# The modulated input of layer 1, made by pairs of token tiles within layer 0's output projection

## The chip, the core and the metric

The kernel runs on one core of one Trainium2 chip. The metric is the device time of one execution in microseconds, as the median of several runs. A profiled execution gives a trace in which TensorE is PE (with its weight loads as PEld), VectorE is DVE, ScalarE is ACT, GpSimd is POOL and SyncE is SP, which issues most DMAs.

## What is computed

Two layers of a hybrid diffusion backbone work on 256 context tokens and 512 latent tokens of width 1024. All is float32. Of the reference, this is what matters here:

```python
def modulate(x, shift, scale):
    return layer_norm(x) * (1.0 + scale) + shift

def hybrid_layer(x, ctx, c, c_ctx, ada_w, ada_b, in_w, ...):
    shift_l, scale_l, gate_l = jnp.split((silu(c) @ ada_w + ada_b)[:, None, :], 3, axis=-1)
    shift_c, scale_c, gate_c = jnp.split(silu(c_ctx) @ ada_w + ada_b, 3, axis=-1)
    pl = split_cols(modulate(x, shift_l, scale_l) @ in_w, IN_SPLITS)
    pc = split_cols(modulate(ctx, shift_c, scale_c) @ in_w, IN_SPLITS)
    ...                                   # four mixers, latent and context
    x_new = post_norm(ALPHA * x + gate_l * merge_branches(outs_l, ..., out_w), ln_g, ln_b)
    ...                                   # the same for the context, in layer 0
    return x_new, ctx_new
```

`merge_branches` ends with `y @ out_w`, the output projection. `post_norm` is a LayerNorm with gain and bias. So at the border of the two layers each token goes through: output projection, gate, residual, LayerNorm with gain (the new x), a plain LayerNorm, scale and shift (the modulated input), and then the first projection of layer 1.

## The kernel before

The 768 tokens are six tiles of 128 (`h[0]` to `h[5]`); tiles 0 and 1 are context (segment 0), tiles 2 to 5 latent (segment 1), and the two segments have their own scale, shift and gate. Each matmul of two float32 operands is made as three, of a high part and a low part of each (hi x hi, hi x lo, lo x hi; `mm3`, L302).

The border of the layers runs as follows.

- `out_operands` splits the merged `y` into 16 tiles `xh` of 128x768: eight high parts (ACT) and eight low parts (DVE). The first is `ys[0]`, the second `ys[1]`.
- `out_proj` goes over the six token tiles. For each it makes two halves of 512 columns, of 24 matmuls 128x512 each, in a PSUM bank of the pool `A`; DVE multiplies by the gate (L1525), adds the residual (L1526) and takes statistics (L1528).
- After a tile's two halves come `first(t)` and `second(t-1)`. `first` is the post-LayerNorm: aggregation (L309, L311), a reciprocal root by integer steps on DVE (L270 to L277), two passes of DVE over 128x1024 (L433, L434), and a store of the new x by SP (L1684). `second` is the plain LayerNorm of the tile before: statistics (L426), the same chain, `lnnb` (L430), and one in-place pass of ACT (L431).
- Then, behind the last tile, `make_xhat` runs for each of eight blocks d of 128 channels: six transposes by PE (L601) into two banks, a modulate of the context half on DVE (L462) and of the latent half on ACT (L465), and the split into high and low part (copy on DVE L479 or ACT L476, subtract on DVE L480 or POOL L477). The results are new tiles, `xh` for the 512 latent tokens and `xc` for the 256 context tokens.
- Between those, the last two of six adaLN blocks of layer 1 (numbers 4 and 5, the gate's part) are made: `ada` loads four weight tiles per block (L387), multiplies each (L392), copies the sum to SBUF (ACT, L397, tile `E`), transposes it by four small matmuls (L400) and adds the bias (DVE, L404). `ada` is a generator with five steps per block; `LEAD` says how many steps go first, and how many after each d.
- Layer 1 then begins with the projection `m_stream` (L572), whose weight tiles `wx` are split on ACT (L292) and DVE (L295).

The order of work on each engine is set by a scheduler from the program's order and its buffers; each engine then runs its own list in order. Tiles `wx` have five buffers, which adaLN loads and projection weights share.

Of the kernel before, what the change touches and what calls it, by code (L numbers as in the profile page):

```python
# [18 lines left out]
DEPTH = 2  # L19
# [15 lines left out]
LEAD = (6, 1, 6)  # L35
# [177 lines left out]
class _Kernel:  # L213
# [241 lines left out]
    def make_xhat(self, d, xn, ad, mp):  # L455
# [11 lines left out]
        out = []  # L467
        for _ in range(2):
            if self.xc is None:
                out.append(self.t(self.xp, [128, T], "xh", F32R))  # L470
            else:
                out.append((self.t(self.xc, [128, CTX], "xc", F32R), self.t(self.xp, [128, LAT], "xh", F32R)))
        for s in [slice(0, T)] if self.xc is None else [slice(0, CTX), slice(CTX, T)]:
            h, lo = (self.xtok(x, s) for x in out)
            if d % 2:
                nc.scalar.activation(out=h, in_=m[:, s], func=AF.Copy)  # L476
                nc.gpsimd.tensor_tensor(out=lo, in0=m[:, s], in1=h.bitcast(F32), op=ALU.subtract)  # L477
            else:
                nc.vector.tensor_copy(h, m[:, s])  # L479
                nc.vector.tensor_tensor(out=lo, in0=m[:, s], in1=h.bitcast(F32), op=ALU.subtract)  # L480
        self.xh.append(out[0])
        self.xl.append(out[1])

    @staticmethod
    def xtok(x, s):

        if not isinstance(x, tuple):
            return x[:, s]
        return x[0][:, s] if s.start < CTX else x[1][:, s.start - CTX:s.stop - CTX]
# [1045 lines left out]
def _run_layers(K, only=None):  # L1535
# [4 lines left out]
    xst, xct = ExitStack(), ExitStack()  # L1540
    K.xp, K.xc = xst.enter_context(mk("xh0", 16)), None
# [12 lines left out]
    for l in range(DEPTH):  # L1554
# [55 lines left out]
        xct.close()  # L1610
# [64 lines left out]
        with K.psum(A=(1, 8)):  # L1675
# [10 lines left out]

            def second(t):
                if not last:
                    K.normalise(h[t], 1e-6)
# [3 lines left out]
            if not last:  # L1693
                vec, ad = nxt["vec"], nxt["ad"]
                K.xh, K.xl = [], []
                xst.close()
                K.xp = xst.enter_context(mk(f"xh{l + 1}", 16))
                K.xc = xct.enter_context(mk(f"xc{l + 1}", 16)) if l + 1 == DEPTH - 1 else None
                with mk(f"xn{l}") as xp:
                    more = K.ada(l + 1, ad, vec, xp, range(4, 6))  # L1700
                    for _ in range(LEAD[0]):
                        next(more)
                    for d in range(8):
                        K.make_xhat(d, xn, ad, xp)
                        for _ in range(LEAD[1]):
                            next(more, None)
# [24 lines left out]
```

## Time and profile before

| | us |
|---|---|
| median of three timed runs | 2080.67 |
| lowest, highest | 2078.30, 2081.94 |
| profiled execution | 2077.99 |
| its span in the trace | 2076.2 |
| tile 3's first matmul of layer 0's output projection | at 1139.42 |
| tile 5's first matmul | at 1161.54 |
| end of tile 5's matmuls | at 1172.69 |
| first matmul of layer 1's first projection | at 1202.39 |

Times inside an execution count from the start of the span. "Busy" is time in which an engine executes; a bracket after an instruction of the trace tells how long its engine had been idle and what it had waited for. The granted clock of PE is a share of its full speed: 1.00 is 2.4 GHz, 0.50 is 1.2 GHz.

### The profile page before, as it was taken

How to read it: one execution, taken by the hardware profiler on the slowest of the kernel's cores; microseconds unless marked ns; L12 is line 12 of the kernel's file. 1: busy time of each engine (PE TensorE's matmuls, PEld its weight loads, DVE VectorE, ACT ScalarE, POOL GpSimd, SP SyncE). 2: the span in 40 equal slices, each digit the busy share in tenths (PEclk: the TensorE clock that was granted, in tenths of full speed). 3: DMA queues.
4: the chain of work that ended last, by engine and by line, in shares of the span. 5: the costliest groups of instructions: out<-in, count | busy, mean ns of one | idle time of the engine just before them, and what ended most of it. 6: DMA issues, size and time to landing. Idle time of an engine off the chain costs nothing. (4 is left out here: it accounts for less than half of the span.)

```text
span 2076.2 us, 46214 instructions
## 1 busy us (share of the span) xinstructions
PE 1900.8 (92%) x19886; PEld 1580.3 (76%) x19886; DVE 1156.2 (56%) x2471; ACT 816.1 (39%) x1649; POOL 180.3 (9%) x303
## 2 busy tenths in 40 slices
PE   6899999888899999999788879999988999999877
PEld 4778978667789998888676677878877777777556
DVE  5554453576434433443878865453686444455677
ACT  3354463565423332332122236463575333333220
POOL 1000000001200000000130010000102000000130
PEclk9899999998899999999999988999999999999999
DMA  7110123220222222223743220111102222232651
GB/s 277 43 31 29 57 87 96 78 67 22 62 79 74 81 73 73 73 73 119 252 147 115 100 66 21 43 43 31 43 21 80 78 93 79 78 91 75 217 184 41
DMA packets 62613, 176.03 MB, mean 85 GB/s; under 512 B 7448, under 2 KB 12232, under 8 KB 62408
## 3 DMA queue, kind: packets, MB, share of 16 engines
q1 hardware_dynamic: 47144, 139.93, 21.4%
q10 hardware_dynamic: 13824, 27.90, 3.9%
q0 software_dynamic: 1440, 5.24, 0.6%
q8 instruction: 156, 2.56, 0.5%
q14 instruction: 49, 0.40, 0.1%
HBM read 145.50 MB, written 27.55 MB: 83 GB/s over the span
## 5 line engine op out<-in xcount | busy, mean ns | idle before, releaser
L302 PE MATMUL ps<-xh,wx 128*128 128x384 f32 (+2 forms) x3096 | 691.7, 368 | 4.5 <-issue 1.8
L302 PEld LDWEIGHTS ps<-xh,wx 128*128 128x128 f32 x3096 | 532.1, 189 | 65.7 <-issue 8.3
L292 ACT ACTIVATE wx<-wx 128x1024 fp32r<-128x1024 f32 (+2 forms) x94 | 98.3, 1046 | 303.5 <-PE ps L302 212.3
L295 DVE TENSOR_TENSOR wx<-wx,wx 128x1024 fp32r<-128x1024 f32 (+2 forms) x94 | 113.5, 1207 | 140.9 <-ACT wx L292 138.8
L650 DVE TENSOR_REDUCE nmax<-ps 128x1 f32<-128x768 f32 (+1 forms) x160 | 134.6, 846 | 56.7 <-PE ps L647 55.7
L572 PE MATMUL ps<-wx,xh 128*128 128x256 f32 (+1 forms) x1200 | 156.4, 289 | 7.6 <-DVE mu L1001 6.7
L572 PEld LDWEIGHTS ps<-wx,xh 128*128 128x128 f32 x1200 | 151.9, 192 | 9.6 <-ACT xc L476 6.7
L302 PE MATMUL ps<-xh,wb 128*128 128x384 f32 (+1 forms) x576 | 131.5, 379 | 28.7 <-DVE th L1484 20.7
L539 PE MATMUL ps<-wx,xh 128*128 128x256 f32 x960 | 141.1, 301 | 14.6 <-DVE oth L1418 7.3
L647 PE MATMUL ps<-qk,qk 128*128 128x384 f32 (+1 forms) x504 | 134.9, 371 | 17.1 <-ACT E L653 16.9
L653 ACT ACTIVATE E<-ps,nmax 128x768 f32<-128x768 f32 (+1 forms) x160 | 130.3, 816 | 45.4 <-DVE nmax L650 41.6
L539 PEld LDWEIGHTS ps<-wx,xh 128*128 128x128 f32 x960 | 129.7, 203 | 20.2 <-DVE oth L1418 7.7
L302 PEld LDWEIGHTS ps<-xh,wb 128*128 128x128 f32 x576 | 105.6, 198 | 51.3 <-DVE th L1484 15.3
L671 ACT ACTIVATE PH<-ps 128x512 f32<-128x512 f32 x156 | 91.1, 596 | 73.4 <-PE ps L669 72.9
L647 PEld LDWEIGHTS ps<-qk,qk 128*128 128x128 f32 x504 | 83.9, 195 | 40.8 <-ACT E L653 28.4
L669 PE MATMUL ps<-cstalways,E 128*128 128x128 f32 x624 | 102.6, 287 | 2.6 <-ACT PH L671 1.4
L1444 ACT ACTIVATE mth<-ps,hmb 128x384 f32<-128x384 f32 (+1 forms) x96 | 58.5, 609 | 112.7 <-PE ps L302 111.1
L669 PEld LDWEIGHTS ps<-cstalways,E 128*128 128x128 f32 x624 | 76.5, 147 | 16.6 <-ACT PH L671 5.2
L694 PE MATMUL ps<-PH,V 128*64 128x256 f32 x624 | 84.3, 397 | 3.7 <-ACT PH L671 3.4
L629 DVE TENSOR_TENSOR qk<-ps,qk 32x256 fp32r<-32x256 f32 (+5 forms) x104 | 59.3, 575 | 43.4 <-ACT qk L628 41.7
L295 DVE TENSOR_TENSOR wx<-wf,wx 128x1024 fp32r<-128x1024 f32 (+2 forms) x34 | 40.0, 1178 | 62.4 <-PE ps L302 33.8
L694 PEld LDWEIGHTS ps<-PH,V 128*64 128x64 f32 x624 | 40.5, 139 | 34.6 <-ACT PH L671 13.4
(325 smaller groups left out, 2784.5 us busy)
## 6 DMA issues: line engine op xcount, KB each, us to landing
wx<-in_inw_dram SPq DMA_DIRECT2D x88, 512.0 KB, 3.7
wf<-in_inw_dram SPq DMA_DIRECT2D x30, 512.0 KB, 3.6
wf<-in_adaw_dram SPq DMA_DIRECT2D x24, 512.0 KB, 3.5
gd<-mth ACTq DMA_DIRECT2D x32, 384.0 KB, 2.6
th<-gd SPq DMA_DIRECT2D x32, 384.0 KB, 3.1
adaw<-in_adaw_dram SPq DMA_DIRECT2D x16, 512.0 KB, 10.2
wx<-in_outw_dram SPq DMA_DIRECT2D x16, 512.0 KB, 4.8
wb<-in_brw_dram SPq DMA_DIRECT2D x32, 256.0 KB, 3.6
```

The source lines that it names most:

```text
L292: nc.scalar.activation(out=hi[:, :n], in_=raw[:, :n], func=AF.Copy)
L295: eng.tensor_tensor(out=lo[:, :n], in0=raw[:, :n], in1=hi[:, :n].bitcast(F32), op=ALU.subtract)
L302: self.nc.tensor.matmul(o, lhsT=w, rhs=x[:, s] if s is not None else x, start=first and p == 0, stop=last and p == 2)
L539: self.nc.tensor.matmul(ps[:, j * n:j * n + n], lhsT=self.xtok(x[k], s), rhs=w, start=k == 0 and p == 0 and j == 0, stop=k == 7 and p == 2 ...
L572: self.nc.tensor.matmul(ps, lhsT=self.xtok(x[k], s), rhs=w[:, c], start=k == 0 and p == 0 and head, stop=k == 7 and p == 2 and (tail or t ...
L629: nc.vector.tensor_tensor(out=lo[r, s], in0=ps[r], in1=hi[r, s].bitcast(F32), op=ALU.subtract)
L647: nc.tensor.matmul(o, lhsT=qt[:n, q], rhs=kt[:n, s], start=i == 0, stop=i == len(passes) - 1)
L650: nc.vector.tensor_reduce(out=nm, in_=v, axis=AX.X if ctx else AX.XY, op=ALU.max, negate=True)
L653: nc.scalar.activation(out=self.halves(e[:, :n], v), in_=v, func=AF.Exp, bias=nm, accum_out=den)
L669: nc.tensor.transpose(pt[:, c:c + 128], e[:, (k0 + k) * 128:(k0 + k) * 128 + 128], self.ident)
L671: nc.scalar.activation(out=hi, in_=pt, func=AF.Copy)
L694: nc.tensor.matmul(po[64 * (kk % 2):64 * (kk % 2) + 64, :n], lhsT=v2(kk), rhs=x[:, s], start=j == 0 and k < 2, stop=j == len(groups) - 1 a ...
```

## The change

`make_xhat` no longer runs at the border. In its place `xhat_pair` makes the modulated input of two token tiles at once, and is called in `second(t)` for each odd t: for tiles 0 and 1 after tile 2's matmuls, for 2 and 3 after tile 4's, for 4 and 5 at the end. For each block d it makes two transposes (now L608), one modulate on ACT (128x256, L485) into a tile `mt` of four buffers, a copy on ACT (L489; on DVE, L487, for the last pair) and a subtract on POOL (L490; on DVE for odd d of the last pair). The results are written into the columns of `ys` that this pair's output projection has already read, so no new tiles are made, and the pools `xh1` and `xc1` are gone. The adaLN blocks 4 and 5 are stepped in `second`, three steps at a time, in a PSUM bank of their own (`D`), and the output projection of layer 0 keeps seven banks in `A`. `make_xhat` is left for layer 0's input alone, where it does what it did. Lines below L490 stand seven further down in the changed kernel (L572 is L579).

```diff
-LEAD = (6, 1, 6)
+LEAD = (0, 3, 6)
...
+    def xhat_pair(self, tt, xn, ad, mp, xh, xl, end):
+
+        nc = self.nc
+        i = 0 if tt[0] < NCT else 1
+        s = slice(tt[0] * 128, tt[-1] * 128 + 128)
+        for d in range(8):
+            ps, _ = self.tok_T(lambda t: xn[t][:, d * 128:(d + 1) * 128], 128, tt, "A")
+            m = self.t(mp, [128, 256], "mt", bufs=4)
+            nc.scalar.activation(out=m, in_=ps, func=AF.Identity, scale=ad[:, 2 * d, i:i + 1], bias=ad[:, 2 * d + 1, i:i + 1])
+            if end:
+                nc.vector.tensor_copy(xh[d][:, s], m)
             else:
...
+                nc.scalar.activation(out=xh[d][:, s], in_=m, func=AF.Copy)
+            (nc.vector if end and d % 2 else nc.gpsimd).tensor_tensor(out=xl[d][:, s], in0=m, in1=xh[d][:, s].bitcast(F32),
+                                                                      op=ALU.subtract)
...
-        with K.psum(A=(1, 8)):
+        with K.psum(**(dict(A=(1, 8)) if last else dict(A=(1, 7), D=(1, 1)))):
+            xp = None if last else mkr(f"xn{l}")
             ys = K.out_operands(y, len(qt) * 128)
...
+            if last:
+                more = None
+            else:
+                more = K.with_bank(K.ada(l + 1, nxt["ad"], nxt["vec"], xp, range(4, 6)), "D")
+
             def second(t):
-                if not last:
-                    K.normalise(h[t], 1e-6)
+                if last:
+                    return
+                K.normalise(h[t], 1e-6)
+                end = t == qt[-1]
+                for _ in range(LEAD[1] if t else 0):
+                    next(more, None)
+                if t % 2:
+
+                    K.xhat_pair((t - 1, t), xn, nxt["ad"], xp, *ys, end)
             with mk(f"ow{l}") as owp:
                 ws.append(K.out_weights(l, 1, owp))
                 K.out_proj(ys, ws, qt, gates_, h, first, second)
             if not last:
+                run(more)
                 vec, ad = nxt["vec"], nxt["ad"]
-                K.xh, K.xl = [], []
-                xst.close()
-                K.xp = xst.enter_context(mk(f"xh{l + 1}", 16))
-                K.xc = xct.enter_context(mk(f"xc{l + 1}", 16)) if l + 1 == DEPTH - 1 else None
-                with mk(f"xn{l}") as xp:
-                    more = K.ada(l + 1, ad, vec, xp, range(4, 6))
-                    for _ in range(LEAD[0]):
-                        next(more)
-                    for d in range(8):
-                        K.make_xhat(d, xn, ad, xp)
-                        for _ in range(LEAD[1]):
-                            next(more, None)
-                    run(more)
+                K.xh, K.xl = ys
```

How the instructions stand on the engines, in three places. In each row the tile written stands left of the arrow, the tiles read right of it; `ow0hi`, `ow1lo` and the like are the output projection's weights, `cstalways` holds the identity for transposes, `cs` the conditioning vectors, and the numbers behind a name tell its buffers apart.

On PE, from the end of tile 2 to the beginning of tile 3 of the output projection, the kernel before has:

```order
L302 MATMUL ps_2078_12685<-ow1hi_2049_12469,xh_2025_12415 128x512
L302 MATMUL ps_2078_12685<-ow1lo_2050_12470,xh_2025_12415 128x512
L302 MATMUL ps_2078_12685<-ow1hi_2049_12469,xh_2026_12416 128x512
L302 MATMUL ps_2091_12758<-ow0hi_2028_12423,xh_2011_12387 128x512
L302 MATMUL ps_2091_12758<-ow0lo_2029_12424,xh_2011_12387 128x512
```

The last two rows are tile 3's. The changed kernel has at the same place:

```order
L302 MATMUL ps_2078_12691<-ow1hi_2049_12475,xh_2026_12422 128x512
L392 MATMUL ps_2090_12763<-wx_2091_12764,cs_45_118 32x256 x4
L608 MATMUL ps_2092_12770<-cstalways_43_113,h0_1850_11641 128x128
...
L392 MATMUL ps_2090_12763<-wx_2140_13042,cs_45_118 32x256 x4
L400 MATMUL ps_2142_13050<-sum4_46_121,E_2141_13048 128x2 x4
L392 MATMUL ps_2174_13217<-wx_2175_13218,cs_45_118 32x256 x4
...
L400 MATMUL ps_2202_13324<-sum4_46_121,E_2201_13322 128x2 x4
...
L608 MATMUL ps_2106_12819<-cstalways_43_113,h1_1851_11643 128x128
L302 MATMUL ps_2109_12827<-ow0hi_2028_12429,xh_2011_12393 128x512
```

Both adaLN blocks and all 16 transposes of tiles 0 and 1 have moved between tile 2 and tile 3. Tile 3's first bank is one that the second L485 has read.

On ACT, from the plain LayerNorm of tile 0 on, the kernel before has:

```order
L431 ACTIVATE h0_1850_11641<-h0_1850_11641,lnnb_2074_12652,lnrs_2072_12639 128x1024
L431 ACTIVATE h1_1851_11643<-h1_1851_11643,lnnb_2089_12754,lnrs_2087_12741 128x1024
L431 ACTIVATE h2_1852_11645<-h2_1852_11645,lnnb_2104_12856,lnrs_2102_12843 128x1024
L431 ACTIVATE h3_1853_11647<-h3_1853_11647,lnnb_2119_12958,lnrs_2117_12945 128x1024
L397 ACTIVATE E_2167_13179<-ps_2141_13097 128x512
```

and the changed kernel:

```order
L431 ACTIVATE h0_1850_11641<-h0_1850_11641,lnnb_2074_12658,lnrs_2072_12645 128x1024
L397 ACTIVATE E_2141_13048<-ps_2090_12763 128x512
L397 ACTIVATE E_2201_13322<-ps_2174_13217 128x512
L431 ACTIVATE h1_1851_11643<-h1_1851_11643,lnnb_2089_12760,lnrs_2087_12747 128x1024
L292 ACTIVATE wx_2208_13372<-wx_2207_13371 128x1024
L485 ACTIVATE mt_2093_12773<-ps_2092_12770,ada_671_3177 128x256
L485 ACTIVATE mt_2095_12780<-ps_2094_12777,ada_671_3177 128x256
L489 ACTIVATE xh_2011_12393<-mt_2093_12773 128x256
```

The adaLN copies now stand ahead of tile 1's normalise, and a weight split of layer 1 and the modulates behind it.

On PE, from the end of tile 5 to layer 1's first projection, the kernel before has:

```order
L302 MATMUL ps_2123_12991<-ow1hi_2049_12469,xh_2026_12416 128x512
L392 MATMUL ps_2141_13097<-wx_2142_13098,cs_45_118 32x256 x4
...
L601 MATMUL ps_2146_13117<-cstalways_43_113,h0_1850_11641 128x128
...
L601 MATMUL ps_2202_13284<-cstalways_43_113,h5_1855_11651 128x128
L400 MATMUL ps_2210_13312<-sum4_46_121,E_2209_13310 128x2 x4
L572 MATMUL ps_2214_13357<-wx_2216_13359,xh_2149_13128 128x256
```

and the changed kernel:

```order
L302 MATMUL ps_2162_13141<-ow1hi_2049_12475,xh_2026_12422 128x512
L608 MATMUL ps_2184_13259<-cstalways_43_113,h4_1854_11649 128x128
...
L608 MATMUL ps_2196_13301<-cstalways_43_113,h5_1855_11651 128x128
L608 MATMUL ps_2198_13308<-cstalways_43_113,h4_1854_11649 128x128
L608 MATMUL ps_2198_13308<-cstalways_43_113,h5_1855_11651 128x128
L579 MATMUL ps_2206_13370<-wx_2208_13372,xh_2011_12393 128x256
```

Of 48 transposes 16 are left at the end. The 16 of tiles 2 and 3 stand between tile 4 and tile 5 in the same way as those of 0 and 1 do between tile 2 and tile 3, without adaLN.

## Rows read from the trace of the kernel before

**Rows 1.** The page, engine totals: busy us, share of the span, instructions.

```profile
PE 1900.8 (92%) x19886; PEld 1580.3 (76%) x19886; DVE 1156.2 (56%) x2471; ACT 816.1 (39%) x1649; POOL 180.3 (9%) x303
```

**Rows 2.** Timeline of PE: start, us, engine, line, operation, count, [idle before, releaser].

```profile
1102.68 0.77 PE L302 MATMUL ps<-ow0hi,xh 128*128 128x512 f32 x1 [5.35 <-issue]
...
1139.42 0.40 PE L302 MATMUL ps<-ow0hi,xh 128*128 128x512 f32 x1
...
1161.54 0.39 PE L302 MATMUL ps<-ow0hi,xh 128*128 128x512 f32 x1
...
1172.69 1.50 PE L392 MATMUL ps<-wx,cs 128*32 128x256 f32 x24
1174.12 1.09 PE L601 MATMUL ps<-cstalways,h 128*128 128x128 f32 x8
...
1176.56 1.05 PE L400 MATMUL ps<-sum,E 128*128 128x2 f32 x8 [0.19 <-ACT E L397]
...
1202.39 14.38 PE L572 MATMUL ps<-wx,xh 128*128 128x256 f32 x96 [6.68 <-DVE mu L1001]
```

**Rows 3.** Stretches: length, busy PE, PEld, DVE, ACT, POOL, granted clock, DMA share, GB/s.

```profile
1102.68:1109.18 6.50, 6.05 (x13) 4.39 (x14) 6.43 (x6) 4.75 (x5) 0.00 (x0) 0.50 0.63 204
1109.50:1116.00 6.50, 6.50 (x30) 5.31 (x29) 4.46 (x6) 2.12 (x2) 0.00 (x0) 1.00 0.95 349
1172.69:1202.39 29.70, 17.04 (x129) 10.88 (x129) 26.75 (x85) 14.55 (x22) 6.61 (x10) 0.76 0.50 173
1182.00:1184.00 2.00, 2.00 (x24) 0.93 (x20) 2.00 (x6) 1.06 (x1) 0.00 (x0) 0.50 0.28 113
1202.39:1208.50 6.11, 6.11 (x29) 6.11 (x30) 2.07 (x6) 0.31 (x1) 1.84 (x2) 0.51 0.01 3
1208.50:1216.60 8.10, 8.10 (x69) 8.10 (x69) 1.06 (x1) 0.93 (x1) 0.00 (x0) 1.00 0.20 55
```

**Rows 4.** Timeline of DVE between 1139 and 1205.

```profile
1145.43 1.28 DVE L434 SCALAR_TENSOR_TENSOR h<-h,lnrs,lnb 128x1024 f32<-128x1024 f32 x1
...
1175.49 0.24 DVE L479 CAST xc<-mt 128x256 fp32r<-128x256 f32 x1
...
1180.03 0.21 DVE L404 TENSOR_SCALAR ada<-ps,pp 128x2 f32<-128x2 f32 x1
...
1182.65 0.69 DVE L426 BATCH_NORM_STATS2 lnst<-h 128x6 f32<-128x512 f32 x1
...
1185.05 0.20 DVE L309 BATCH_NORM_AGGREGATE lnmv<-lnst 128x2 f32<-128x12 f32 x1
...
1203.00 1.25 DVE L1006 TENSOR_SCALAR c<-pp 128x2 f32<-128x2 f32 x1
```

**Rows 5.** Timeline of ACT between 1139 and 1249.

```profile
1147.49 1.24 ACT L431 ACTIVATE h<-h,lnnb,lnrs 128x1024 f32<-128x1024 f32 x1 [9.81 <-DVE lnnb L430]
...
1169.69 1.25 ACT L431 ACTIVATE h<-h,lnnb,lnrs 128x1024 f32<-128x1024 f32 x1 [9.90 <-DVE lnnb L430]
...
1175.91 0.60 ACT L397 ACTIVATE E<-ps 128x512 f32<-128x512 f32 x1 [4.97 <-PE ps L392]
...
1187.80 1.24 ACT L431 ACTIVATE h<-h,lnnb,lnrs 128x1024 f32<-128x1024 f32 x1 [1.27 <-DVE lnnb L430]
1188.94 1.04 ACT L292 ACTIVATE wx<-wx 128x1024 fp32r<-128x1024 f32 x1
...
1192.40 0.78 ACT L465 ACTIVATE mt<-ps,ada 128x512 f32<-128x512 f32 x1
...
1248.65 0.37 ACT L628 ACTIVATE qk<-ps 128x256 fp32r<-128x256 f32 x1
```

**Rows 6.** Timeline of POOL between 1178 and 1205.

```profile
1178.55 0.72 POOL L477 TENSOR_TENSOR xc<-mt,xc 128x256 fp32r<-128x256 f32 x1 [77.79 <-ACT xc L476]
...
1202.95 1.28 POOL L477 TENSOR_TENSOR xh<-mt,xh 128x512 fp32r<-128x512 f32 x1
```

**Rows 7.** DMA issues from 1095 to 1240: KB each, median us from issue to landing.

```profile
wx<-in_adaw_dram SPq DMA_DIRECT2D x8, 512.0 KB, 5.2
```

More of the change, by code (lines that the diff above doesn't have):

```diff
@@ L466, in make_xhat @@
                                      bias=ad[:, 2 * d + 1, 1:2])
[L467 to L470, printed above, removed]
-            else:
[L472 to L480, printed above, removed]
@@ L481, in make_xhat @@
-        self.xh.append(out[0])
-        self.xl.append(out[1])
+        h, lo = (self.t(self.xp, [128, T], "xh", F32R) for _ in range(2))
+        if d % 2:
+            nc.scalar.activation(out=h, in_=m, func=AF.Copy)
+            nc.gpsimd.tensor_tensor(out=lo, in0=m, in1=h.bitcast(F32), op=ALU.subtract)
+        else:
+            nc.vector.tensor_copy(h, m)
+            nc.vector.tensor_tensor(out=lo, in0=m, in1=h.bitcast(F32), op=ALU.subtract)
+        self.xh.append(h)
+        self.xl.append(lo)
@@ L484, in xtok @@
     @staticmethod
     def xtok(x, s):
-        if not isinstance(x, tuple):
-            return x[:, s]
-        return x[0][:, s] if s.start < CTX else x[1][:, s.start - CTX:s.stop - CTX]
+        return x[:, s]
     def take_w(self):
@@ L1539, in _run_layers @@
     ad = K.new_ada()
-    xst, xct = ExitStack(), ExitStack()
-    K.xp, K.xc = xst.enter_context(mk("xh0", 16)), None
+    xst = ExitStack()
+    K.xp = xst.enter_context(mk("xh0", 16))
     with mk("xn0") as xp0, K.psum(A=(1, 8)):
@@ L1609, in _run_layers @@
         left = ExitStack()
-        xct.close()
         K.rp = mkr(f"rw{l}")
@@ L1685, in first @@
                                   K.xs[t * 128:(t + 1) * 128], in_=h[t])
+            if last:
+                more = None
+            else:
+                more = K.with_bank(K.ada(l + 1, nxt["ad"], nxt["vec"], xp, range(4, 6)), "D")
             def second(t):
-                if not last:
-                    K.normalise(h[t], 1e-6)
+                if last:
[6 more added lines that the diff above has]
+                    K.xhat_pair((t - 1, t), xn, nxt["ad"], xp, *ys, end)
             with mk(f"ow{l}") as owp:
```

## The prediction

> **What bounds the kernel now.** I read the page's engine totals first: PE is busy 1900.8 of 2076.2 us [rows 1], so the question for any change is where PE idles near it, and whether the change fills that or makes more of it. Then PE's own timeline around the end of layer 0. The last three token tiles run without a break: tile 3 begins at 1139.42, tile 5 at 1161.54, and tile 5's last matmul gives way to adaLN matmuls at 1172.69 [rows 2]. So the six tiles, about 11.06 us each ((1161.54 - 1139.42) / 2), are bound by PE alone, and DVE and ACT work behind them for nothing. Next the stretch between the output projection and layer 1's first projection matmul at 1202.39: 29.70 us, of which PE is busy 17.04, much of that at half clock (0.50 in 1182 to 1184), while DVE is busy 26.75 [rows 2, 3]. DVE, not PE, sets that end. It is the only place the change can win; the tiles are where it can lose.
>
> The sum is made against the profiled execution, 2077.99 us (span 2076.2). It lies 2.7 us under the median of the three timed runs, 2080.67; I add the sum to that median.
>
> **The tail (a gain).** Before, 29.7 us lie between tile 5 and layer 1's first projection [rows 3]. After, only the pair (4,5) is left there, and adaLN blocks and the weight splits stand earlier. I build it from the undisturbed tile 2, whose matmuls ended at 1139.42: the post-LayerNorm of that tile (L434) ended at 1145.43 + 1.28 = 1146.71 [rows 4], 7.3 us after. For tile 5 in the new order follow two statistics of 0.69 each, 1.4 [rows 4], and from the aggregation at 1185.05 to the end of ACT's normalise at 1187.80 + 1.24 = 1189.04 another 4.0 [rows 4, 5]: 12.7 us after tile 5. Then the eight steps of `xhat_pair`. Layer 1's first projection waits, for its bank, on the last of eight ACT modulates of 128x256 from PSUM. No row shows that form; the nearest are a 128x256 eviction at 0.37 and the 128x512 modulate at 0.78 [rows 5]. I take 0.45, near the one of equal size: 3.6, and 0.5 for the transposes and hand-over ahead, 4.1. The four `mt` buffers come free behind a DVE cast (0.24) and, for even d, a POOL subtract (0.72) [rows 4, 6]; four POOL subtracts are 2.9, inside the eight modulates, so they just fit. If the casts and subtracts run slower the steps take 6. I take 5: the tail is 17.7, the gain 29.7 - 17.7 = **12.0** (11.0 to 12.9).
>
> A row that speaks for the upper end: an instruction of DVE on 128x2, L1006, took 1.25 us beside a POOL subtract of 1.28 that had begun 0.05 before it [rows 4, 6]. The Trainium skill, in "Advanced Engine Details and Errata", section "VectorE Performance Modes" (Mode Summary), says that VectorE's second SBUF port is shared with GpSimd, so that an instruction using both ports and one of GpSimd block each other. That row agrees with it in kind. By it alone, if each POOL subtract held up a cast, the eight steps would take the 6 of my upper bound, and the time would be 2098; I stay at 5, since the row is one instruction.
>
> **Between tile 2 and tile 3 (a loss).** PE is in order, and its new order puts the adaLN matmuls and both tiles' transposes between tile 2 and tile 3. The transposes of h1 need ACT's in-place normalise of h1, which DVE's chain for tile 1 releases; that chain is woven with tile 2's post-LayerNorm, so it ends after tile 2. In the trace it ended at 1147.49 + 1.24 = 1148.73, 9.3 us after tile 2's last matmul [rows 5]. That wait is free today, since PE is already in tile 3. Four of adaLN's L404 now stand in the same DVE chain: 4 x 0.21 [rows 4], less what overlaps, 0.5. A weight split of 1.04 [rows 5] stands on ACT between that normalise and the modulates; 0.3 for the first transposes; tile 3's first matmul waits for the bank that the second modulate frees, two at 0.45, 0.9; hand-overs 0.4. Together **12.5**. The adaLN loads also bound it: five of eight are loaded early, three wait for their buffers until PE has used the first ones at the end of tile 2, and take 5.2 to land [rows 7]; then the copy of 0.60 on ACT [rows 5], ahead of h1's normalise. That is some 7 us after tile 2 if they land as quickly as before, 8.5 if they queue, against 8.1 for the DVE chain, so it adds 0 to 1. Bounds 11.5 to 13.5. SP stores h1 between those loads; that tile is finished by then, so nothing queues behind it.
>
> **Between tile 4 and tile 5 (a loss).** The same without adaLN: h3's normalise ended at 1169.69 + 1.25 = 1170.94, 9.4 us after tile 4's last matmul at 1161.54 [rows 2, 5]; transposes 0.3, two modulates 0.9, hand-over 0.2: **10.8** (10.3 to 11.5). Between tiles 3 and 4, 0 and 1, 1 and 2 nothing is placed, so no wait there. The 16 transposes and their modulates, casts and subtracts that don't hold the next tile run beside its 11 us of matmuls: ACT 8 x (0.45 + 0.3), POOL 8 x 0.72, both under 11, no cost. The bank taken from the tiles leaves seven, where one half tile needs one for 5.5 us: no cost.
>
> **Clock (a loss).** After 5.35 us of idle PE ran at half its clock (0.50) from 1102.68 to 1109.18, and after 6.68 us of idle at 0.51 from 1202.39 to 1208.50, then at 1.00 [rows 2, 3]. One 128x512 took 0.77 there against 0.40 in full clock [rows 2], so 6.1 to 6.5 us at half cost 6.5 x (1 - 0.40 / 0.77) = 3.1. Tile 5 begins after some 8 us of idle: 3. Tile 3's gap has adaLN matmuls and transposes within it, so PE may come back sooner or not: 0 to 3, and as the half clock within the busier stretch of 1182 to 1184 shows that such sprinkling doesn't keep it, 2. Together **5** (0 to 6). Layer 1's first projection starts at half clock before and begins after a like wait now: no difference.
>
> The rest of layer 1 keeps its instructions and waits; context and latent operands now share a tile, whose slices are read as before: 0.
>
> Sum: 12.5 + 10.8 + 5 - 12.0 = **+16.3**; 2080.67 + 16.3 = **2097.0 us**. On the profiled execution it would be 2094.3.
>
> **Rivals.**
> (1) PE doesn't wait between the tiles, and only the work is moved: then the tail's 12.0 is gained, and PE's own work between the tiles is added: 64 adaLN matmuls recorded, 24 in 1.50, 4.0; 32 transposes, 8 in 1.09, 4.4; two sum groups of 1.05, 2.1 [rows 2]; 10.5. That gives -1.5, 2079.2. The Trainium skill, in "Perfetto Trace Analysis" (Optimization Strategy), says that where a kernel has regimes with different most-contended engines, interleaving them may gain. The tail is DVE's and the tiles are PE's, so by that rule the time would come out here. Against it: the two normalises end 9.3 and 9.4 us after the tile whose end they would have to beat [rows 5], and PE passes nothing by. It would need a normalise that ends before its tile does.
> (2) The clock holds, or returns at once, in both gaps: +11.3, 2092.0. For it: transposes and adaLN matmuls are work; against it, the two restarts [rows 3].
> (3) The upper ends meet, with adaLN loads late (+1), the gap before tile 5 at 11.5, half clock in all of both restarts (+1), and the last pair's steps at 6 to 8 (+1 to +3): +20 to +22, up to 2103. The price decides at POOL: if each subtract takes 1.28 instead of 0.72 [rows 6], the ring of four sets the pace.
>
> **How the numbers follow.** My forecast 0.60, (2) 0.17, (3) 0.11, (1) 0.10, the change undone somewhere I don't see 0.02. A measurement tells 0.2% (4.2 us) from no change, so (1) is mostly the same, with 0.03 of it faster; of the last, 0.01 each. Faster 0.04, same 0.08, slower 0.88. The range goes from the low ends without a clock loss, 11.5 + 10.3 - 12.9 = +8.9, 2089.5, lowered to 2089, to (3), 2103; it leaves out (1).
>
> **What would show it.** In PE's timeline after: a gap of about 12.5 between the last matmul of tile 2 and the first of tile 3, with h1's normalise (L431) ending 9 to 10 us into it; none before tile 4; a gap of 10.8 before tile 5, then some 6 us at half clock; and 17.7 from tile 5's last matmul to layer 1's first projection. I am wrong if PE starts tile 3 with h1 still unready, if the tail stays near 29.7 or falls far under 17, or if layer 1's later stages change length.

## The result, and the profile after

The changed kernel takes 2093.11 us (median of 2090.71 to 2097.04) against 2081.31 for the kernel before: a ratio of 1.0065, interval 1.0047 to 1.0082. It is slower, by some 0.65%. The prediction was 2097, range 2089 to 2103. Its profiled execution took 2090.71, span 2089.0; that of the kernel before 2077.99 and 2076.2, so the traces differ by 12.8 us. The experiments' ratios are of fast runs alone, against the kernel before timed in the same series (medians 2078.14, 2078.26 and 2076.72); one execution of 3509 us (`e1_late`) and one of 8754 us (the kernel before) are not in them.

The rows of PE's timeline that answer to [rows 2] show where. The columns are start, us, engine, line, operation, count, and in brackets the idle time before it and its releaser.

```profile
1101.36 0.76 PE L302 MATMUL ps<-ow0hi,xh 128*128 128x512 f32 x1 [5.34 <-issue]
...
1137.81 0.64 PE L392 MATMUL ps<-wx,cs 128*32 128x256 f32 x8
1138.38 0.98 PE L608 MATMUL ps<-cstalways,h 128*128 128x128 f32 x7
1139.29 1.50 PE L392 MATMUL ps<-wx,cs 128*32 128x256 f32 x24
1141.51 1.05 PE L400 MATMUL ps<-sum,E 128*128 128x2 f32 x8 [0.72 <-ACT E L397]
1143.65 2.00 PE L392 MATMUL ps<-wx,cs 128*32 128x256 f32 x24 [1.08 <-DVE ada L404]
1145.90 1.08 PE L392 MATMUL ps<-wx,cs 128*32 128x256 f32 x8 [0.26 <-DMA wx<-in_adaw_dram]
1147.76 1.87 PE L400 MATMUL ps<-sum,E 128*128 128x2 f32 x8 [0.78 <-ACT E L397]
1149.49 2.16 PE L608 MATMUL ps<-cstalways,h 128*128 128x128 f32 x9
1151.30 0.78 PE L302 MATMUL ps<-ow0hi,xh 128*128 128x512 f32 x1
...
1175.21 1.27 PE L608 MATMUL ps<-cstalways,h 128*128 128x128 f32 x7
1184.61 2.18 PE L608 MATMUL ps<-cstalways,h 128*128 128x128 f32 x9 [8.13 <-ACT h L431]
1186.44 0.78 PE L302 MATMUL ps<-ow0hi,xh 128*128 128x512 f32 x1
...
1198.58 0.39 PE L302 MATMUL ps<-ow1hi,xh 128*128 128x512 f32 x1
1208.21 1.75 PE L608 MATMUL ps<-cstalways,h 128*128 128x128 f32 x7 [9.25 <-ACT h L431]
1211.56 2.18 PE L608 MATMUL ps<-cstalways,h 128*128 128x128 f32 x9 [1.59 <-ACT h L431]
1216.87 0.58 PE L579 MATMUL ps<-wx,xh 128*128 128x256 f32 x1 [3.12 <-ACT mt L485]
```

Tile 2 ends at 1137.81 and tile 3 begins at 1151.30; before, these were the same moment, 1139.42. Tile 4 ends at 1175.21 and tile 5 begins at 1186.44; before, 1161.54. Ahead of tile 5, the 8.13 us of idle in front of the second batch of transposes name the culprit, ACT's normalise of h (L431). Ahead of tile 3 it is less plain: PE idles 2.84 us in all, in four pieces that end with adaLN's copies (L397), DVE's L404 and a load, and it goes from adaLN's last sums (L400) to the second batch of transposes without idle. And layer 1's first projection (L579) begins 17.90 us after the last projection matmul ends (1198.58 + 0.39), against 29.63 before, counted in the same way (1172.76 to 1202.39).

The stretches answer to [rows 3]: length, busy PE, PEld, DVE, ACT, POOL with counts, granted clock, DMA share, GB/s. The first two are the two gaps, the third and fourth tiles 3 and 4 after the first gap, the fifth and sixth tile 5 with the transposes before it, then the last stretch and layer 1's first projection.

```profile
1137.81:1151.30 13.49, 10.65 (x97) 6.86 (x97) 10.36 (x43) 4.58 (x8) 0.00 (x0) 0.76 0.70 235
1175.21:1186.44 11.23, 2.97 (x17) 2.55 (x16) 8.38 (x34) 2.50 (x5) 0.00 (x0) 0.66 0.11 47
1151.30:1155.06 3.76, 3.76 (x11) 2.99 (x10) 0.10 (x1) 3.76 (x12) 3.48 (x5) 0.51 0.00 0
1155.06:1175.21 20.15, 20.15 (x90) 16.37 (x89) 13.23 (x41) 3.31 (x6) 2.24 (x4) 1.00 0.15 49
1184.61:1189.30 4.69, 4.69 (x16) 4.12 (x17) 0.00 (x0) 4.12 (x11) 2.62 (x4) 0.52 0.00 1
1189.30:1198.97 9.67, 9.66 (x42) 7.55 (x41) 2.08 (x3) 2.08 (x6) 3.11 (x5) 1.00 0.00 0
1198.97:1216.87 17.90, 3.94 (x17) 3.14 (x17) 13.99 (x64) 6.50 (x10) 2.33 (x6) 0.61 0.19 62
1216.87:1219.87 3.00, 3.00 (x14) 3.00 (x15) 1.87 (x4) 0.00 (x0) 1.06 (x2) 0.51 0.41 163
1219.87:1222.87 3.00, 3.00 (x27) 3.00 (x27) 0.00 (x0) 0.00 (x0) 0.00 (x0) 1.00 0.57 164
```

The ledger between the traces, in us, with the term of the prediction beside each:

| part | measured | predicted |
|---|---|---|
| gap ahead of tile 3 | +13.49 | +12.5 |
| gap ahead of tile 5 | +11.23 | +10.8 |
| tiles 3 and 4 slower (23.91 against 22.12) | +1.79 | +2 |
| tile 5 slower (12.53 against 11.22) | +1.31 | +3 |
| last stretch (17.90 against 29.63) | -11.73 | -12.0 |
| tiles 0 to 2 | -0.29 | 0 |
| **first projection matmul to layer 1's first matmul** (115.51 against 99.71) | **+15.80** | +16.3 |
| layer 0 up to there (1101.36 against 1102.68) | -1.32 | 0 |
| layer 1 (872.13 against 873.81) | -1.68 | 0 |
| span | +12.80 | +16.3 |

### The profile page after: what moved, and what is told of

It is laid out like the page before. It is cut to its first block, busy times and chain, and to the rows that moved or that the text cites. A ratio compares the mean times of both kernels' runs of the same rounds, so it can differ in the third digit from the quotient of the medians.

```text
span 2089.0 us, 46267 instructions
## 1 busy us (share of the span) xinstructions
PE 1893.6 (91%) x19886; PEld 1573.7 (75%) x19886; DVE 1146.0 (55%) x2459; ACT 823.5 (39%) x1673; POOL 187.7 (9%) x315
## 5 line engine op out<-in xcount | busy, mean ns | idle before, releaser
L302 PE MATMUL ps<-xh,wx 128*128 128x384 f32 (+2 forms) x3264 | 716.1, 364 | 3.8 <-ACT mth L1451 1.7
L302 PEld LDWEIGHTS ps<-xh,wx 128*128 128x128 f32 x3264 | 552.9, 189 | 67.1 <-issue 9.3
L292 ACT ACTIVATE wx<-wx 128x1024 fp32r<-128x1024 f32 (+2 forms) x94 | 98.3, 1046 | 300.5 <-PE ps L302 208.7
L295 DVE TENSOR_TENSOR wx<-wx,wx 128x1024 fp32r<-128x1024 f32 (+2 forms) x94 | 113.5, 1208 | 138.3 <-ACT wx L292 137.7
L579 PE MATMUL ps<-wx,xh 128*128 128x256 f32 (+1 forms) x1344 | 169.6, 287 | 4.7 <-ACT mt L485 3.1
L579 PEld LDWEIGHTS ps<-wx,xh 128*128 128x128 f32 x1344 | 167.0, 190 | 7.6 <-ACT mt L485 3.5
L302 PE MATMUL ps<-xh,wb 128*128 128x384 f32 (+1 forms) x576 | 130.9, 377 | 30.4 <-DVE th L1491 20.9
L546 PE MATMUL ps<-wx,xh 128*128 128x256 f32 x960 | 141.4, 301 | 14.8 <-DVE oth L1425 7.3
L654 PE MATMUL ps<-qk,qk 128*128 128x384 f32 (+1 forms) x504 | 135.1, 372 | 16.7 <-ACT E L660 16.4
L546 PEld LDWEIGHTS ps<-wx,xh 128*128 128x128 f32 x960 | 129.9, 203 | 20.3 <-DVE oth L1425 7.7
L654 PEld LDWEIGHTS ps<-qk,qk 128*128 128x128 f32 x504 | 84.4, 196 | 40.0 <-ACT E L660 28.7
L295 DVE TENSOR_TENSOR wx<-wf,wx 128x1024 fp32r<-128x1024 f32 (+2 forms) x34 | 40.0, 1177 | 60.0 <-PE ps L302 33.8
```

The lines of the kernel that those rows point to most:

```text
L292: nc.scalar.activation(out=hi[:, :n], in_=raw[:, :n], func=AF.Copy)
L295: eng.tensor_tensor(out=lo[:, :n], in0=raw[:, :n], in1=hi[:, :n].bitcast(F32), op=ALU.subtract)
L302: self.nc.tensor.matmul(o, lhsT=w, rhs=x[:, s] if s is not None else x, start=first and p == 0, stop=last and p == 2)
L546: self.nc.tensor.matmul(ps[:, j * n:j * n + n], lhsT=self.xtok(x[k], s), rhs=w, start=k == 0 and p == 0 and j == 0, stop=k == 7 and p == 2 ...
L579: self.nc.tensor.matmul(ps, lhsT=self.xtok(x[k], s), rhs=w[:, c], start=k == 0 and p == 0 and head, stop=k == 7 and p == 2 and (tail or t ...
L654: nc.tensor.matmul(o, lhsT=qt[:n, q], rhs=kt[:n, s], start=i == 0, stop=i == len(passes) - 1)
```

## The experiments

The code of layer 0 up to the projection is the same in every kernel here, yet the projection's first matmul began anywhere from 1100.0 to 1110.3 in the fourteen traces. The granted clock up to there goes with it: its mean was 0.97 in the three that began first and 0.96 in the two that began last. So the whole time of one execution tells little of a change of some us. I compare the **window**, from the projection's first matmul to layer 1's first, divided into the tiles (with the stops between them) and the last stretch (from the end of the projection's last matmul); the timed ratio stands beside it where there is one.

| kernel | window | tiles | last stretch | ratio to before (interval) |
|---|---|---|---|---|
| before | 99.71 | 70.08 | 29.63 | |
| after | 115.51 | 97.61 | 17.90 | 1.0065 (1.0047 to 1.0082) |
| e1_late | 98.76 | 75.04 | 23.72 | 1.0006 (0.9989 to 1.0023) |
| e4_late_ada_end | 94.67 | 71.55 | 23.12 | 0.9989 (0.9971 to 1.0007) |
| e5_direct | 108.73 | 91.03 | 17.70 | 1.0067 (1.0044 to 1.0090) |
| e5_again | 106.49 | 88.79 | 17.70 | 1.0038 (1.0023 to 1.0053) |
| e3_one_pair | 105.91 | 85.02 | 20.89 | 1.0033 (1.0021 to 1.0045) |
| e11_ada_layer1 | 92.29 | 71.39 | 20.90 | 1.0158 (1.0135 to 1.0182) |
| e9_late_ada_early | 99.22 | 78.31 | 20.91 | one execution |
| e10_ada_only | 101.09 | 73.26 | 27.83 | one execution |
| e10_again | 101.41 | 73.58 | 27.83 | 0.9997 (0.9981 to 1.0014) |
| e16_no_sub | 96.26 | 78.36 | 17.90 | one execution |
| e15_warm | 114.84 | 96.94 | 17.90 | one execution |
| e6_direct_late | 97.41 | 72.81 | 24.60 | 1.0016 (1.0001 to 1.0031) |

My theory was that PE's **wait** for a normalise loses what the shorter end gains; the rival, that the **moved work** on PE costs that wherever it stands.

### Each pair one tile later

```diff
-                if t % 2:
-                    K.xhat_pair((t - 1, t), xn, nxt["ad"], xp, *ys, end)
+                if t in (2, 4):
+                    K.xhat_pair((t - 2, t - 1), xn, nxt["ad"], xp, *ys, False)
+                if end:
+                    K.xhat_pair((t - 1, t), xn, nxt["ad"], xp, *ys, end)
```

> The changed kernel with one edit: each pair is made one token tile later, (0,1) behind tile 3 and (2,3) behind tile 5, so that its normalise is done when PE comes to its transposes. The same PE work stands between tile 2 and layer 1's first projection. Theory 'wait' (the changed kernel loses because PE stops for a normalise, 13.5 us ahead of tile 3 and 11.2 ahead of tile 5, not because of the work moved): no stop over 3 us between tiles 2 and 5, tiles 2 to 5 longer than before only by the moved PE work, about 6 us, the last stretch 18 to 20 us against 29.7 before: 2075 to 2078 us. Rival 'moved work' (the transposes and adaLN matmuls between the tiles cost what was lost, wherever they stand): only the transposes of (2,3) leave the tiles, 2 us: about 2091.

Measured: the ratio is 1.0006, 12 us less than the changed kernel. That is over what the theory gave (2075 to 2078 is 0.9970 to 0.9984 of the 2081.31 that it was counted from), and under the rival's 2091 (1.0047). No stop is left between the tiles, and they are 4.96 us longer than before, which is PE's own moved work (16 transposes 1.97, adaLN the rest). The scheduler put only 32 of adaLN's 64 matmuls between the tiles here; the others stand behind tile 5, with the transposes of (2,3). Two runs below price the moved work in full, with no stop: all of adaLN and one pair make the tiles 8.23 us longer (`e9_late_ada_early`), one pair alone 1.47 (`e4_late_ada_end`). So some 9.7 of the 27.5 us by which the changed kernel's tiles grew are moved work, which is less than the 11.7 gained at the end. The other 17.8 are waiting and half clock: in this sense the theory of the wait holds. But the last stretch took 23.7, not 18 to 20; runs below take that apart.

### The same, with adaLN behind the last pair

```diff
-LEAD = (0, 3, 6)
+LEAD = (0, 0, 6)
```

> As the run before, and the adaLN blocks 4 and 5 stepped only behind the last pair. Theory 'wait': tile 3 follows tile 2 at once; between tiles 3 and 4 only 16 transposes, 2 to 3.5 us; none before tile 5; the 16 transposes of (2,3) and the adaLN matmuls fall into the time in which PE waits for the last normalise, so the last stretch is 18 to 21 us: 2071 to 2075. Rival 'moved work': 8 us less than the changed kernel, about 2085, if adaLN costs at the end what it cost between the tiles.

Measured: the window is 94.67, the shortest but one. The tiles (71.55) came out a little under what was expected, the last stretch (23.12) over it. Layer 1's first projection then stopped once more, for 2.06 us behind its first matmul, for a weight split that came late: ACT's part of it (L292) waited 2.36 for its load, which stands behind adaLN's loads in the queue. The ratio, 0.9989, can't be told from 1. What was expected, 2071 to 2075, is 0.9950 to 0.9970 of the 2081.31 that it was counted from, just below the interval: the gain that I had expected did not come.

### The second layer norm straight behind the first

```diff
                 nc.sync.dma_start(out=K.out[(t - NCT) * 128:(t - NCT + 1) * 128] if last else
                                   K.xs[t * 128:(t + 1) * 128], in_=h[t])
+                if not last:
+                    K.normalise(h[t], 1e-6)
...
             def second(t):
                 if last:
                     return
-                K.normalise(h[t], 1e-6)
```

> The changed kernel with one edit: the plain LayerNorm of a tile is written straight behind its post-LayerNorm, not behind that of the next tile; the pairs and adaLN stay where the program has them. The transposes still stand between tiles 2 and 3 and tiles 4 and 5. Theory 'wait': the gap ahead of tile 3 shrinks from 13.5 to about 8 (tile 1's normalise is still woven with tile 2's work on DVE, and four L404 wait for adaLN), that ahead of tile 5 from 11.2 to about 6: 2081 to 2085. Rival 'moved work': the same PE work is between the tiles, so within 2 us of the changed kernel, 2091 to 2095.

> e5_direct once more, beside the kernel before. In its trace the stops had shrunk (9.4 and 8.7) and the stretch from the projection's first matmul to layer 1's was 108.7 against 115.5 in the changed kernel, but its time was the same. If the stages decide: before plus 9, 2086 to 2089. If something outside these stages is longer in this kernel (layer 0 ended 7 us later in that trace): 2091 to 2094 again, and layer 0 ends late again.

Measured: the gaps shrank from 13.5 to 9.4 and from 11.2 to 8.7 in the first trace, less than I thought, since four L404 wait in the DVE chain for PE's sums. One thing moved that I had not meant to move: the scheduler put most of one adaLN block (22 matmuls and its sums) into the second gap, so the 4.1 us saved ahead of tile 3 are not the earlier normalise's alone. Ahead of tile 5 the reading is clean, in two rows of PE in the first trace:

```profile
1179.44 1.06 PE L392 MATMUL ps<-wx,cs 128*32 128x256 f32 x14
...
1184.58 2.18 PE L608 MATMUL ps<-cstalways,h 128*128 128x128 f32 x9 [2.32 <-ACT h L431]
```

More PE work stands in that gap than in the changed kernel; the normalise ended 6.8 instead of 9.3 us after tile 4, the idle for it fell from 8.13 to 2.32, and the gap is 2.5 shorter. The first set of times (2092.23, four runs) stands with the rival, and the second (2085.16, seven runs) between the two: 6.9 us over the kernel before, as the second trace's window says (+6.8). The projection began 7.2 and 6.9 us later than in the trace of the changed kernel. The window is what speaks here; the two ratios, 1.0067 and 1.0038, are the price of judging a 0.3% change by few runs.

### Only one pair between the tiles

```diff
-                if t % 2:
-                    K.xhat_pair((t - 1, t), xn, nxt["ad"], xp, *ys, end)
+                if t == 1:
+                    K.xhat_pair((0, 1), xn, nxt["ad"], xp, *ys, False)
+                if end:
+                    K.xhat_pair((2, 3), xn, nxt["ad"], xp, *ys, False)
+                    K.xhat_pair((4, 5), xn, nxt["ad"], xp, *ys, end)
```

> The changed kernel with the pair (2,3) made at the end, with (4,5); (0,1) and adaLN as in the changed kernel. It prices the second stop alone. Theory 'wait': the gap ahead of tile 3 stays 13 to 14, tiles 3, 4 and 5 run in one piece, so 11.2 of gap and 1.3 of half clock are saved; the pair's 16 transposes fit into PE's wait in the last stretch, its modulates and copies on ACT (6.5 us) mostly as well, so that stretch grows by 0 to 6 from 18: 2081 to 2087. Rival 'moved work': 2.2 us of transposes move from one place to another, 2091 to 2093.

Measured: tiles 12.6 shorter than in the changed kernel (11.2 of gap and 1.3 of slow clock, as expected), the last stretch 3.0 longer. The window, 105.91, is in the middle of what the theory expected (103 to 109); the ratio, 1.0033, is a little over it (2081 to 2087 is 0.9999 to 1.0027 of the 2081.31 that it was counted from). So the pair (2,3) between the tiles saved 3.0 us at the end and cost 12.6.

### Where the three microseconds at the end come from

The last stretch is 17.90 where only the pair (4,5) stands in it, and 20.89, 20.90 and 20.91 in three kernels where (2,3) stands there too. I suspected ACT at first, which has 6 us of modulates and copies for (2,3).

`e9_late_ada_early` is `e1_late` with adaLN block 4 behind tile 1 and block 5 behind tile 2:

```diff
-                for _ in range(LEAD[1] if t else 0):
+                for _ in range(9 if t in (0, 1) else 1 if t == 2 else 0):
```

> Pairs one tile later, adaLN block 4 behind tile 1 and block 5 behind tile 2, so that no adaLN is left behind tile 5. In e1_late the last stretch was 23.8 us and PE's sum matmul (L400) waited 5.3 for ACT's copy of the adaLN sum. Theory 'DVE's L404 of a late adaLN block held up the last tile's chain': the last stretch falls to 18 to 19, the tiles grow by 8 us of PE work: 96 to 98 us from the projection's first matmul to layer 1's. Rival 'the modulates of (2,3) on ACT hold up the last tile': the last stretch stays 22 to 24.

Measured: the last stretch 20.9, between what the two theories expected. So 2.8 of the 23.7 in `e1_late` came with adaLN's late block: in that trace four L404, some 0.5 us, and two weight splits (L295, 1.63 and 1.23) stand in DVE's chain behind tile 5, and here none does. DVE did not wait for them. The other 3.0 show in DVE's timeline of this kernel, together with POOL's one row in the stretch:

```profile
1190.33 6.49 POOL L490 TENSOR_TENSOR xh<-mt,xh 128x256 fp32r<-128x256 f32 x8 [17.17 <-ACT xh L489]
```

```profile
1191.14 1.68 DVE L433 SCALAR_TENSOR_TENSOR h<-h,lnmv,lng 128x1024 f32<-128x1024 f32 x1
...
1194.82 0.65 DVE L275 TENSOR_TENSOR rsq<-lnrs 128x1 f32<-128x1 f32 x1
1195.39 0.15 DVE L277 SCALAR_TENSOR_TENSOR lnrs<-rsq,lnrs 128x1 f32<-128x1 f32 x1
1195.51 0.65 DVE L276 SCALAR_TENSOR_TENSOR rsq<-rsq,lnve 128x1 f32<-128x1 f32 x1
1196.08 0.15 DVE L275 TENSOR_TENSOR rsq<-lnrs 128x1 f32<-128x1 f32 x1
1196.19 0.65 DVE L277 SCALAR_TENSOR_TENSOR lnrs<-rsq,lnrs 128x1 f32<-128x1 f32 x1
1196.76 0.15 DVE L276 SCALAR_TENSOR_TENSOR rsq<-rsq,lnve 128x1 f32<-128x1 f32 x1
1196.87 0.16 DVE L275 TENSOR_TENSOR rsq<-lnrs 128x1 f32<-128x1 f32 x1
```

Until POOL's eight subtracts end at 1196.82, every second two-operand instruction of one element takes 0.65, the one between 0.15; the next after them takes 0.16. The decisive run leaves these eight subtracts out (so the low part of two tiles is not computed):

```diff
-            (nc.vector if end and d % 2 else nc.gpsimd).tensor_tensor(out=xl[d][:, s], in0=m, in1=xh[d][:, s].bitcast(F32),
-                                                                      op=ALU.subtract)
+            if tt[0] != 2:
+                (nc.vector if end and d % 2 else nc.gpsimd).tensor_tensor(out=xl[d][:, s], in0=m, in1=xh[d][:, s].bitcast(F32),
+                                                                          op=ALU.subtract)
```

> e9_late_ada_early without the eight POOL subtracts of the pair (2,3): the low part of these two tiles is left out, so this kernel computes less. In e9 the last stretch was 21.0 us against 18.0 in the changed kernel, and tile 4's plain LayerNorm ended 3 us later after tile 5; two-operand DVE instructions of one element took 0.65 instead of 0.16 while POOL subtracted. Theory 'POOL's subtracts hold up DVE's chain': these rows are 0.16 again and the last stretch is 17.9 to 18.5. Rival 'ACT's modulates and copies of (2,3) hold up the normalise': it stays 20.5 to 21.5.

DVE's timeline in the chain of tile 5 in that run:

```profile
1190.32 0.15 DVE L276 SCALAR_TENSOR_TENSOR rsq<-rsq,lnve 128x1 f32<-128x1 f32 x1
1190.44 0.16 DVE L275 TENSOR_TENSOR rsq<-lnrs 128x1 f32<-128x1 f32 x1
...
1190.63 0.16 DVE L276 SCALAR_TENSOR_TENSOR rsq<-rsq,lnve 128x1 f32<-128x1 f32 x1
```

Measured: in the same chain no such row is above 0.16, and the last stretch is 17.90, as in the changed kernel, although ACT still does all of (2,3)'s work. So POOL's subtracts beside DVE's chain cost 3.0 us, and ACT's work nothing. The Trainium skill, "GPSIMD Engine Reference", section "1. Specifications", says that GpSimd shares its SBUF interfaces with VectorE and gets in the way of instructions of VectorE with two SBUF inputs; the trace agrees, 0.65 against 0.16 for every second one of such rows.

### What adaLN's place is worth

`e10_ada_only` is the kernel before with adaLN alone stepped between the tiles:

```diff
             def second(t):
                 if not last:
                     K.normalise(h[t], 1e-6)
+                    for _ in range(3 if t else 0):
+                        next(more, None)
...
-                    more = K.ada(l + 1, ad, vec, xp, range(4, 6))
```

> The kernel before with one edit: adaLN blocks 4 and 5 are stepped between the tiles of the output projection (in a bank of their own), make_xhat stays where it was, behind tile 5. It splits the gain of 11.7 in the last stretch (29.7 before, 18.0 after). Theory 'most of the gain comes from taking adaLN out of DVE's way': the last stretch 23 to 25. Rival 'most comes from the modulated input of tiles 0 to 3 being made earlier': 27 to 29.

> e10_ada_only once more, timed. Its one time was 7 us under the kernel before although the stretch from the projection's first matmul to layer 1's was 101.1 against 99.7. If the stretch decides: 0 to 3 us over the kernel before. If adaLN's new place gives something in layer 1: 5 to 8 us under it again.

Measured: the last stretch 27.83 in both traces, 1.8 of the 11.7 that the change gains there. But only one of the two adaLN blocks has left it. The other still stands there, as PE's row behind tile 5 in the second trace shows:

```profile
1179.17 1.93 PE L392 MATMUL ps<-wx,cs 128*32 128x256 f32 x32
```

So 1.8 is what one block's leaving gives, and 9.9 are left for the second block and the earlier tiles 0 to 3 together. With the pairs late, both blocks' leaving gave 2.2 (23.12 in `e4_late_ada_end`, 20.90 in `e11_ada_layer1`) and one block's 2.8 (`e1_late`, `e9_late_ada_early`). By all of these most of the gain is the earlier pairs': the rival, not my theory; the exact split is not shown. The tiles grow by 3.2 to 3.5, so the edit by itself loses 1.4 to 1.7 in the window. Ten runs have a median of 2076.59 where the single time was 2070.8, a ratio of 0.9997. In both traces layer 1 was shorter than in the one trace of the kernel before (865.2 and 868.5 against 873.8), at a mean granted clock of 0.98 and 0.97 against 0.96.

`e11_ada_layer1` takes adaLN out of the border altogether, into layer 1's attention, with the pairs one tile later as in `e1_late` and no step of adaLN left in `second`. The part that differs from `e1_late`, cut:

```diff
...
         def fill():
             yield from K.rwkv_inputs(l)
-            if l == 0:
-                yield from K.ada(0, ad, vec, K.ep, range(4, 6))
+            yield from K.ada(l, ad, vec, K.ep, range(4, 6))
...
-                for _ in range(LEAD[1] if t else 0):
+                for _ in range(0):
...
-                run(more)
```

> Pairs one tile later as in e1_late, and the adaLN blocks 4 and 5 of layer 1 taken out of the border and made as filler beside layer 1's attention, where the first four of layer 0's neighbours are made. Between tile 2 and layer 1 only transposes are added. Theory 'what is left is adaLN in the DVE chain and in PE's row': from the projection's first matmul to layer 1's first 90 to 91 us (70.0 for the tiles, 2 for 16 transposes, 18 to 19 for the end) against 99.7 before and 98.8 in e1_late; layer 1 longer by 0 to 6, so 2069 to 2075. Rival 'adaLN costs PE its 6 us wherever it stands': layer 1 longer by the full 6: 2074 to 2076, no different from e1_late within the measurement.

Measured: the window is the shortest of all, 92.29, but the kernel is 31 us slower than before. Two groups of PE's matmuls in layer 1 tell where. The first fence is of `e11_ada_layer1`, the second of `e1_late`: line, duration min/median/max in ns, first and last start; L654 is attention's score matmul, L546 the gate's projection.

```profile
L654 PE MATMUL ps<-qk,qk x224: 331/339/689, 1244.4 to 1557.2; 128*128 128x384 f32 x112
L546 PE MATMUL ps<-wx,xh x384: 274/283/582, 1564.5 to 1645.3; 128*128 128x256 f32 x192
```

```profile
L654 PE MATMUL ps<-qk,qk x224: 331/338/446, 1250.5 to 1567.8; 128*128 128x384 f32 x112
L546 PE MATMUL ps<-wx,xh x384: 274/282/583, 1496.6 to 1614.1; 128*128 128x256 f32 x192
```

In `e1_late` the gate's projection begins 71 us before attention's last score; here it begins after it. The adaLN blocks stand ahead of the gate in the filler (their first matmul comes 296.5 us after layer 1's first, where the gate's came at 296.6 in `e1_late`), and the gate, of which 71 us had run beside attention, came behind it in the open. Layer 1 took 40.9 us more than in `e1_late`, and 38.6 of them are lost before the scan (its first L1250 starts 445.9 us after layer 1's first matmul, against 407.4). Neither the theory nor the rival had this.

### The clock

```diff
+        if tt[0] == 2:
+            keep = self.P("A")
+            for j in range(72):
+                nc.tensor.transpose(keep[:, j % 4 * 128:j % 4 * 128 + 128], xn[2][:, j % 8 * 128:j % 8 * 128 + 128], self.ident)
```

> The changed kernel with 72 transposes of a finished tile ahead of the pair (2,3), into a bank that nobody reads: they fill PE's stop ahead of tile 5. Theory 'the stop costs its length and, through the clock, a slow start of tile 5': the stop stays 11 to 12.5 us, and tile 5's matmuls take 11.2 at full clock instead of 12.5. Rival 'tile 5 is longer for another reason (the modulates and copies beside it)': 12.3 to 12.7 again.

Tile 5 in the changed kernel and then in this one, in the columns of the stretches above:

```profile
1186.44:1198.97 12.53, 12.52 (x50) 9.84 (x48) 2.08 (x3) 4.94 (x14) 5.72 (x8) 0.89 0.00 0
1195.08:1206.41 11.33, 11.33 (x51) 8.94 (x49) 2.08 (x3) 5.13 (x14) 5.75 (x8) 1.00 0.00 1
```

Measured: with PE kept busy in the gap, tile 5 ran at a granted clock of 1.00 in 11.33 us with the same ACT and POOL work beside it; in the changed kernel it took 12.53 at 0.89. The gap stayed, at 10.9. So the clock's share of tile 5 is 1.2 us, shown and not argued, in one execution. The window came out 0.7 under the changed kernel's; the single time, 2105.5, was 15 above that of the changed kernel's trace (2090.71), since in that execution layer 0 took 8 and layer 1 7 us more. Layer 1's mean granted clock was 0.96 there and 0.97 in the changed kernel's trace; more than that I did not follow.

### A version that was meant to beat both

`e6_direct_late` joins the edits of `e4_late_ada_end` and `e5_direct`.

> e4_late_ada_end with the plain LayerNorm written straight behind the post-LayerNorm, as in e5: no stop between the tiles, and tile 4's chain no longer woven with tile 5's at the end. From the projection's first matmul to layer 1's 93 to 95 us (e4: 94.7), with 1 to 2.5 us more in layer 1's first projection where its weights are late behind the adaLN loads, as in e4: 2 to 5 us under the kernel before, 0.9975 to 0.999 of it. Rival 'adaLN in the last stretch takes back what the pairs gave': no different from before, 0.9995 to 1.001.

Measured: the rival. The tiles take 72.8, but the last stretch 24.6, with 2.0 more in layer 1's first projection: PE waits 2.48 for DVE within (2,3)'s transposes, and adaLN's two blocks stand between the normalises of tiles 4 and 5; which of these weighs how much was not separated. The ratio is 1.0016. None of the kernels run beats the kernel before by more than can be measured.

## Why the prediction was right

**The bound.** That PE bounds the tiles and DVE the end held in every run: tiles at 70.1 plus the PE work that is put between them when nothing waits (`e1_late`, `e4_late_ada_end`, `e9_late_ada_early`), the end at 17.7 to 17.9 wherever DVE's chain for the last tiles is undisturbed.

**The tail.** Predicted gain 12.0, measured 11.73. The step that built it from the undisturbed tile 2 [rows 4, 5] was right: tile 5's plain LayerNorm ended at 1210.27 + 1.24, 12.5 us after the last matmul (predicted 12.7). The eight steps took 5.4 until layer 1's first matmul (predicted 5). My own reason for the gain had no split; the runs give 1.8 to 2.8 for adaLN's leaving and the larger part to the earlier pairs. The last row here is the one of tile 5, the first that of tile 3, used below:

```profile
1183.31 1.24 ACT L431 ACTIVATE h<-h,lnnb,lnrs 128x1024 f32<-128x1024 f32 x1 [9.88 <-DVE lnnb L430]
...
1210.27 1.24 ACT L431 ACTIVATE h<-h,lnnb,lnrs 128x1024 f32<-128x1024 f32 x1 [2.11 <-DVE lnnb L430]
```

**Ahead of tile 3.** Predicted 12.5, measured 13.49. The number came near, by a path that was not quite the one in the sum. ACT's rows show the end of the normalise:

```profile
1147.11 0.60 ACT L397 ACTIVATE E<-ps 128x512 f32<-128x512 f32 x1 [5.65 <-PE ps L392]
1147.60 1.23 ACT L431 ACTIVATE h<-h,lnnb,lnrs 128x1024 f32<-128x1024 f32 x1
1148.74 1.04 ACT L292 ACTIVATE wx<-wx 128x1024 fp32r<-128x1024 f32 x1
1149.98 1.02 ACT L485 ACTIVATE mt<-ps,ada 128x256 f32<-128x256 f32 x2 [0.20 <-PE ps L608]
```

The normalise ended 11.0 us after tile 2, where the prediction had looked for 9 to 10. DVE had released it at 1146.93 (L430, 1146.79 + 0.14), but ACT stood at the adaLN copy, which had waited for the last loads and for PE's matmuls on them. The prediction named that second chain and put it at 0 to 1 us; it took 0.7. What the sum did not have is what came after: PE went on to adaLN's last sums (L400, 1147.76) and reached the second batch of transposes from there, without idle, at 1149.49, 0.7 us after the normalise had ended. So at the end of this gap it was adaLN's chain that held PE, the normalise having ended just before, and the weight split of 1.04 that stands in the sum ran beside L400 and cost nothing. That the two nearly cancel is luck. No run takes one of the two chains alone out of this gap. The four L404 were sized wrongly, 0.5 instead of 1.1 (L430 ended 9.1 after tile 2, 8.0 before), since DVE also idled 0.79 for PE's sums. The modulate of 128x256 that no row before showed takes 0.56; the next begins 0.45 to 0.47 after it, so that two took 1.02, against 0.9 taken.

**Ahead of tile 5.** Predicted 10.8, measured 11.23; h3's normalise ended at 1183.31 + 1.24, 9.34 us after tile 4 (9.4 predicted). The rest is transposes at half clock, 2.18 for nine records.

**The clock.** The mis-sized term: 5 predicted, 3.1 measured. It took the time at half clock after a stop from two rows (6.1 and 6.5 us) [rows 3]. After the changed kernel's stops tiles 3 and 5 ran 3.8 and 2.9 us at half clock, the transposes ahead of them running at half clock already, and layer 1's first projection 3.0 instead of 6.1. The prediction had that last as no difference; it is not the change's doing, for `e16_no_sub`, with the same last stretch, ran 5.4 us at half clock there, and its layer 1 (871.9) was as short. What made layer 1 1.68 us shorter than before stays open.

**The sum.** The window grew by 15.80, where 16.3 was predicted. That they are so near is in part luck: the gaps came out 1.4 over, the clock 1.9 under. The traces' 12.80 and the timed ratio's 13.5 are lower, the traces for the 3.0 us outside the window, which are within what executions differ by.

**The rivals.** The first, that PE doesn't wait and the time comes out at 2079, is nearly what `e1_late` is: ratio 1.0006, with an interval that takes in the rival's -1.5 us (0.9993). The condition that the prediction gave for it, a normalise that ends before PE comes to its transposes, is the edit of that run. The second, a clock that holds, had the right direction for part of the term. The third named POOL's subtracts as the point from which the last pair would be slower; they were hardly slower (0.73 to 0.78, against 0.72), but in kernels with (2,3) at the end they cost 3.0 by another way, DVE's chain.

## What to carry to other kernels

An engine that is the bound must find its next instruction ready: before moving work of a slower chain between its pieces, read when that chain ends against when the engine will arrive there, and place the work one piece later if it ends after. Then price what the moved work does to the other engines' chains too: eight POOL subtracts, free by POOL's own busy time, cost 3 us through DVE. And work that fills gaps takes a place that other work had: look at what it pushes out into the open.

## What I had not expected of the hardware

- While POOL ran subtracts of 128x256, DVE instructions of one element per partition with two operands from SBUF took 0.65 instead of 0.16, every second one, and a 128x1024 one 1.68 instead of 1.28; without the subtracts all were back (`e16_no_sub`). POOL lost as well: the subtract beside that 128x1024 instruction took 1.55 instead of 0.72.
- The time at half clock after a stop varied: 6.5 and 6.1 us in the kernel before, 4.7 (1184.61 to 1189.30) and 3.0 in the changed one, 5.4 in `e16_no_sub`; and layer 0, the same instructions in all, ended up to 10 us apart between executions.
